# Three-pass products with the weight's low part last, and a mask moved from TensorE to VectorE

## The chip, the cores and the metric

The kernel runs on one core of one Trainium2 chip. The metric is device time in microseconds, as the median of several runs of the compiled program. The engines are TensorE (PE, with its weight loads shown apart as PEld), VectorE (DVE), ScalarE (ACT), GpSimd (POOL) and the queue that issues most DMAs (SP).

## The reference, cut to what matters

Two transformer blocks run one after the other on 256 tokens of width 1024, all in fp32. The first has a latent attention, a gated recurrence and a gated feed-forward; the second has two masked attentions of eight heads and an expert layer over 16,384 experts.

```
h = rms_norm(x, g_mix);  z = h @ w_in;  a = mla(...);  r = hgrn2(...)
x = x + concat([a, r]) @ w_o
x = x + (silu(rms_norm(x) @ w_gate) * (rms_norm(x) @ w_up)) @ w_down
x = x + sigmoid(rms_norm(x) @ w_ple_gate) * (p @ w_ple_proj)
...
x = x + hybrid_mixer(rms_norm(x))     # scores, causal mask, softmax, twice 8 heads
x = x + peer_ffn(rms_norm(x))         # every one of 128 x 128 expert rows is multiplied
out = rms_norm(x)
```

The mask keeps keys at or before the query; masked scores become minus infinity before the softmax.

## The kernel before, in words

Nearly all of the time goes to fp32 products that are made of three matmuls each in a faster format. Each operand is split into a high part (a rounded copy) and a low part (what the rounding left): `wh`, `wl` for the weight and `xh`, `xl` for the activations. The product is then wl·xh + wh·xl + wh·xh, summed in PSUM.

`unit` (L96) brings one block of a weight, mostly 512 KB: SP issues the load into `wraw`, ACT writes the high part `whi` (L107), and DVE, or POOL for some units, subtracts to give `wlo` (L112). For some units marked "add", ACT writes the negative of the high part and a DMA issued by POOL adds the raw weight (L109, L110). Each of the three buffers exists four times.

`mm3` (L118) issues the three matmuls of one step k in the order wl·xh (L120), wh·xl (L121), wh·xh (L122). `prodT` (L124) makes a tile of 128 outputs by 256 tokens from eight such steps, 24 matmuls in all, then calls `emit`, which reads the sum and often prepares the next layer's operands. `natural` (L147) does the same with tokens on the rows and up to 512 outputs per matmul (L152 to L154); `nat512` calls it with two steps per unit. `half` (L732, w_o), the products of the two branches in the second block, `w_down`, and `experts_in` (L1037, `expert_u`) call `mm3` themselves.

All engines run their instructions in the order in which the program issues them. Work beside the products (the recurrence, the attentions) is a set of generators that `tick` advances a few steps after each tile.

`Norm` (L182) collects the squares of a layer's output while it is made; `sums` (L211) adds them over the partitions by matmuls against two columns of ones (L216), and `spread` (L221) makes the inverse root available along the other axis. In a `prodT` with a `pre` list these two run after the first and the second tile. The first such products are w_in, the gate and up weights, w_ple_gate and w_pq.

The program starts with twelve products of ones (L261), issued before any data has come. Each fp32 product of whole precision shows as two matmul records.

In `attention` (L887), `scores` (L901) computes a head's scores for 128 queries by W keys (128 or 256): one fp32 product (L904), for the second attention two more for the decay (L906, L907), and one that adds the mask as identity times mask (L908). DVE takes the maximum (L910) and scales it (L911), and ACT takes the exponential out of PSUM (L913).

Of the kernel before, what the change touches and what calls it, by code (L numbers as in the profile page):

```python
# [9 lines left out]
F32R = mybir.dt.float32r  # L10
# [3 lines left out]
AF = mybir.ActivationFunctionType  # L14
OP = mybir.AluOpType
AX = mybir.AxisListType
# [3 lines left out]
T = 256  # L20
D = 1024
# [40 lines left out]
def body(tc, a, out, dbg=None):  # L62
    nc = tc.nc
    ctx = ExitStack()
    pool = lambda name, bufs=1, **k: ctx.enter_context(tc.tile_pool(name=name, bufs=bufs, **k))
# [6 lines left out]
    V = nc.vector  # L72
    S = nc.scalar
    G = nc.gpsimd
    PE = nc.tensor
# [48 lines left out]
    def prodT(name, n0, n1, kt, cols, x, emit, steps=0, pool=lambda u: False, pre=(), given=None):  # L124


        xh, xl = x
        held = []
        pre = list(pre)
        for u in range(n0, n1):  # L130
            wh, wl = given if given is not None and u == n0 else unit(a[name][u], (kt, cols), pool(u))
            for c in range(cols // 128):
                p = pmm()
                o = p[:, :T]
                s = slice(c * 128, (c + 1) * 128)
                for k in range(kt):
                    mm3(o, wh[:, k, s], wl[:, k, s], xh[:, k], xl[:, k], k == 0, k == kt - 1)
                held.append((u * (cols // 128) + c, o))
                if pre:
                    pre.pop(0)()  # L140
                if not pre:
                    for i in held:
                        emit(*i)
                    held = []
                tick(steps)

    def natural(p, wh, wl, x, j, kts, first, last, x0=0):  # L147

        xh, xl = x
        s = slice(j * 128, (j + 1) * 128)  # L150
        for k in range(kts):
            PE.matmul(p, xl[:, x0 + k, s], wh[:, k], start=first and k == 0, stop=False)  # L152
            PE.matmul(p, xh[:, x0 + k, s], wl[:, k], start=False, stop=False)  # L153
            PE.matmul(p, xh[:, x0 + k, s], wh[:, k], start=False, stop=last and k == kts - 1)  # L154

    def nat512(name, u0, x, emit, steps=0, pre=(), pool=lambda q: False):
        pj = [pmm(), pmm()]
# [19 lines left out]
    def rstd(r, v, ss, inv, eng=V):  # L177

        eng.tensor_scalar(v, ss, inv, EPS, op0=OP.mult, op1=OP.add)
        G.tensor_tensor(r, v, mhalf.to_broadcast([128, int(r.shape[1])]), op=OP.pow)  # L180

    class Norm:  # L182
# [25 lines left out]
        def make(self, bank):  # L208


            def sums():  # L211
                p = self.p = bank()
                for j in range(2):
                    js = slice(j * 128, (j + 1) * 128)
                    for i, sq in enumerate(self.parts):
                        PE.matmul(p[:, j * 2:j * 2 + 2], sq[:, js], ones[:, 0:2], start=i == 0, stop=i == len(self.parts) - 1)  # L216
                v = st.tile([128, 2], F32, name="nv", bufs=2)
                self.rn = res.tile([128, 2], F32, name="rnat", bufs=2)
                rstd(self.rn, v, p[:, 0:4:2], 1.0 / D)
# [26 lines left out]
    def cc(n):  # L246
        return cst[:, CC[n][0]:CC[n][1]]
# [7 lines left out]
    with tc.tile_pool(name="la", bufs=1) as la, tc.tile_pool(name="pa", bufs=1, space=PSUM) as pa:  # L255
        pax = lambda: pa.tile([128, 512], F32, name="ax", bufs=2)
        pay = lambda: pa.tile([128, 512], F32, name="ay", bufs=3)

        p = pay()
        for _ in range(12):  # L260
            PE.matmul(p[:, 0:128], ones, ones, start=True, stop=True)  # L261
        norm = Norm("g_mix")
        sqx = xb()

# [428 lines left out]
        prodT("w_in", 0, 4, 8, 128, h, emit_z, 4, pre=[steps[0], first_spread], given=unit0, pool=lambda u: u == 2)  # L693
# [38 lines left out]
        def half(k0, x, emit):  # L732
            for n in range(8):
                wh, wl = unit(a["w_o"][n][:, k0:k0 + 4], (4, 128))
                o = pmm()[:, :T]
                for k in range(4):
                    mm3(o, wh[:, k], wl[:, k], x[0][:, k], x[1][:, k], k == 0, k == 3)
                emit(n, o)
                tick(4)

# [72 lines left out]
    with tc.tile_pool(name="lb", bufs=1) as la, tc.tile_pool(name="pb", bufs=1, space=PSUM) as pb:  # L813
# [2 lines left out]
        pao = lambda: pb.tile([128, 512], F32, name="ao", bufs=1)  # L816
        nb = norm
        h = nb.h
        identr = la.tile([128, 128], F32R, name="identr")
        G.tensor_copy(identr, ident)  # L820
        negr = la.tile([128, 256], F32R, name="negr")
        G.tensor_copy(negr, cc("negmask"))
# [64 lines left out]
        def attention(b):  # L887

            q_, k_ = (qk["qa"], qk["ka"]) if b == 0 else (qk["qb"], qk["kb"])
            for j in range(2):  # L890
# [10 lines left out]
                def scores(hh):  # L901
                    rr = slice((hh % 2) * 64, (hh % 2) * 64 + 64)
                    p = psc()
                    PE.matmul(p[:, :W], q_[rr, hh // 2, js], k_[rr, hh // 2, :W], start=True, stop=False)  # L904
                    if b == 1:
                        PE.matmul(p[:, :W], cr[:, js], selr[:, hh, :W], start=False, stop=False)  # L906
                        PE.matmul(p[:, :W], selr[:, hh, js], crn[:, :W], start=False, stop=False)  # L907
# [85 lines left out]
    with tc.tile_pool(name="lp", bufs=1) as la, tc.tile_pool(name="pp", bufs=1, space=PSUM) as pb:  # L993
# [43 lines left out]
        def experts_in(c, how=False):  # L1037

            p = pmm()
            if how == "whole":  # L1040
                raw = st.tile([128, 8, 128], F32, name="wraw", bufs=4)
                nc.sync.dma_start(raw, a["expert_u"][c])
                for k in range(8):
                    PE.matmul(p[:, :T], raw[:, k], xf[:, k], start=k == 0, stop=k == 7)  # L1044
            else:
                hi, lo = unit(a["expert_u"][c], (8, 128), how)
                for k in range(8):
                    mm3(p[:, :T], hi[:, k], lo[:, k], xn[0][:, k], xn[1][:, k], k == 0, k == 7)
# [361 lines left out]
```

## Time and profile before

| what | value |
|---|---|
| median of 3 runs | 1461.62 us (1459.44 to 1462.62) |
| time of the profiled execution | 1456.88 us |
| its span, first to last instruction | 1455.1 us |
| PE busy | 1416.9 us, 97% |
| PEld busy | 1299.6 us, 89% |
| DVE busy | 1009.9 us, 69% |
| ACT busy | 763.4 us, 52% |
| POOL busy | 147.3 us, 10% |
| mean granted TensorE clock | 0.99 |

The busy time of PE holds ends that are modelled and overlap, so what PE does is read better from the distance between the starts of two matmuls. The granted clock is a share of full speed, 2.4 GHz; 0.50 is the lower of its two levels, 1.2 GHz. The profiled execution's own time is 4.74 us below the median of the runs.

### The profile page before, as it was taken

What the parts mean: (1) busy time and instruction counts of PE and PEld (TensorE: products, weight loads), DVE (VectorE), ACT (ScalarE), POOL (GpSimd) and SP (SyncE); (2) the same over time, 40 slices, a digit from 0 to 9 for tenths busy, and PEclk for the clock granted to TensorE, in tenths of its full rate; (3) what the DMA queues carried; (4) which work ended last, traced back from release to release, by engine and by line L of the source; (5) the groups of instructions that cost most, each with busy time, mean ns of one, the idle gap of its engine ahead of it and who ended that gap; (6) DMA issues with size and microseconds to landing.
All of it is one profiled execution on the core that took longest, in us unless ns stands there. A gap on an engine that the chain in (4) does not pass through costs nothing.

```text
span 1455.1 us, 25805 instructions
## 1 busy us (share of the span) xinstructions
PE 1416.9 (97%) x10238; PEld 1299.6 (89%) x10238; DVE 1009.9 (69%) x1792; ACT 763.4 (52%) x1182; POOL 147.3 (10%) x124
## 2 busy tenths in 40 slices
PE   8899999999999999899899999999999999999997
PEld 8796999999988889889899999899999998888886
DVE  6867877765765557796979995655555555577775
ACT  6764654444654444553257775555444444444443
POOL 4222200001100001367300000000000000000000
PEclk9999999999999999999999999999999999999999
DMA  7672566566554334645357777866676676797752
GB/s 232 165 203 59 165 193 187 188 180 190 161 169 132 115 108 142 200 132 160 116 200 250 246 247 258 277 206 210 195 221 215 222 214 192 230 293 217 220 185 92
DMA packets 104713, 275.98 MB, mean 190 GB/s; under 512 B 8464, under 2 KB 42000, under 8 KB 102416
## 3 DMA queue, kind: packets, MB, share of 16 engines
q1 hardware_dynamic: 100848, 252.31, 55.8%
q10 hardware_dynamic: 2304, 16.78, 3.1%
q0 software_dynamic: 1440, 5.24, 2.0%
q8 instruction: 80, 1.31, 0.4%
q14 instruction: 41, 0.34, 0.1%
HBM read 251.23 MB, written 17.83 MB: 185 GB/s over the span
## 4 chain that ended last, share of the span: by engine, by line
PE 84%; DVE 7%; ACT 3%; issue 3%; DMA 2%; POOL 1%; SPq 0%; POOLq 0%; ACTq 0%; DVEq 0%
PE mm L120 15%; PE mm L121 15%; PE mm L122 15%; PE ax L1233 8%; PE ax L1235 8%; PE ax L1234 8%; PE ax L1206 3%; PE mm L1044 2%; DVE wlo L112 1%; PE sc L904 1%; PE mm L152 1%; PE mm L154 1%; PE mm L153 1%; DVE hl L175 1%; DVE xnt L1062 1%
## 5 line engine op out<-in xcount | busy, mean ns | idle before, releaser
L112 DVE TENSOR_TENSOR wlo<-wraw,whi 128x1024 fp32r<-128x1024 f32 (+3 forms) x408 | 485.5, 1190 | 292.9 <-ACT whi L107 290.3
L107 ACT ACTIVATE whi<-wraw 128x1024 fp32r<-128x1024 f32 (+3 forms) x447 | 459.5, 1029 | 367.3 <-issue 158.1
L120 PE MATMUL mm<-hh,wlo 128*128 128x256 f32 x1928 | 548.7, 285 | 9.5 <-ACT hh L174 3.1
L121 PE MATMUL mm<-hl,whi 128*128 128x256 f32 x1928 | 541.7, 281 | 3.2 <-DVE hl L175 3.2
L122 PE MATMUL mm<-hh,whi 128*128 128x256 f32 x1928 | 540.5, 280 | 0.0
L120 PEld LDWEIGHTS mm<-hh,wlo 128*128 128x128 f32 x1928 | 365.0, 189 | 14.3 <-ACT hh L174 3.5
L121 PEld LDWEIGHTS mm<-hl,whi 128*128 128x128 f32 x1928 | 367.6, 191 | 7.8 <-DVE hl L175 4.5
L122 PEld LDWEIGHTS mm<-hh,whi 128*128 128x128 f32 x1928 | 365.4, 190 | 0.1
L1233 PE MATMUL ax<-whi,al 128*128 128x512 f32 x512 | 202.9, 397 | 0.5 <-DVE al L171 0.5
L1235 PE MATMUL ax<-whi,ah 128*128 128x512 f32 x512 | 202.6, 396 | 0.0
L1234 PE MATMUL ax<-wlo,ah 128*128 128x512 f32 x512 | 202.4, 395 | 0.0
L1050 ACT ACTIVATE hs<-mm 128x256 f32<-128x256 f32 x128 | 49.2, 384 | 159.4 <-PE mm L122 146.6
L1235 PEld LDWEIGHTS ax<-whi,ah 128*128 128x128 f32 x512 | 96.3, 188 | 22.9
L1233 PEld LDWEIGHTS ax<-whi,al 128*128 128x128 f32 x512 | 96.3, 188 | 21.0 <-PE mm L122 0.7
L1234 PEld LDWEIGHTS ax<-wlo,ah 128*128 128x128 f32 x512 | 96.4, 188 | 20.3
L112 POOL TENSOR_TENSOR wlo<-wraw,whi 128x1024 fp32r<-128x1024 f32 x29 | 73.0, 2525 | 216.7 <-ACT whi L107 216.6
L1249 POOL TENSOR_TENSOR ff<-fss 128x1 f32<-128x1 f32 x2 | 1.4, 698 | 730.9 <-ACT fsq L1244 730.9
L1199 DVE TENSOR_TENSOR oA<-one,g 128x3072 bf16<-128x3072 bf16 x32 | 56.0, 1755 | 0.6
L170 ACT ACTIVATE ah<-am 128x256 fp32r<-128x256 f32 x128 | 51.2, 401 | 5.0 <-DVE am L1222 5.0
L171 DVE TENSOR_TENSOR al<-am,ah 128x256 fp32r<-128x256 f32 x128 | 53.5, 418 | 0.2 <-ACT ah L170 0.2
L1206 PE MATMUL ax<-oA,one 128*128 128x128 bf16 x768 | 50.7, 219 | 1.6 <-DVE oA L1199 1.6
L122 PE MATMUL mm<-acth,whi 128*128 128x256 f32 x176 | 49.3, 280 | 0.0
(415 smaller groups left out, 1758.5 us busy)
## 6 DMA issues: line engine op xcount, KB each, us to landing
wraw<-in_expert_u_dram SPq DMA_DIRECT2D x128, 512.0 KB, 3.6
wraw<-in_expert_v_dram SPq DMA_DIRECT2D x128, 512.0 KB, 3.6
wraw<-in_w_gu_dram SPq DMA_DIRECT2D x44, 512.0 KB, 3.7
wraw<-in_w_in_nat_dram SPq DMA_DIRECT2D x24, 512.0 KB, 3.6
wraw<-in_w_down_dram SPq DMA_DIRECT2D x16, 512.0 KB, 3.6
wraw<-in_w_in_g_dram SPq DMA_DIRECT2D x16, 512.0 KB, 3.6
wraw<-in_w_pq_dram SPq DMA_DIRECT2D x16, 512.0 KB, 3.5
gd<-hh ACTq DMA_DIRECT2D x8, 1024.0 KB, 4.7
```

Of the source, the lines that this page charges most:

```text
L107: S.activation(hi[:, s], raw[:, s], AF.Copy)
L112: (G if pool else V).tensor_tensor(lo[:, s], raw[:, s], hi[:, s].bitcast(F32), op=OP.subtract)
L120: PE.matmul(o, wl, xh, start=first, stop=False)
L121: PE.matmul(o, wh, xl, start=False, stop=False)
L122: PE.matmul(o, wh, xh, start=False, stop=last)
L170: S.activation(hi, src, AF.Copy)
L171: V.tensor_tensor(lo, src, hi.bitcast(F32), op=OP.subtract)
L1199: V.tensor_tensor(A3, ow[:, :, 0:1].to_broadcast(s3), g3[:, qs].rearrange("p q k b -> p (q k) b")[:, :, None].to_broadcast([128, PAIRS * 3 ...
L1206: PE.matmul(p[:, i * 128:(i + 1) * 128], ow[:, q, 1, b::2], A3[:, q, k, b::2], start=k == 0, stop=k == 2)
L1233: PE.matmul(o, al[:, js], hi[:, ns], start=c == 0, stop=False)
L1234: PE.matmul(o, ah[:, js], lo[:, ns], start=False, stop=False)
L1235: PE.matmul(o, ah[:, js], hi[:, ns], start=False, stop=c == 127)
```

## The change

- `mm3s` takes all steps of a tile at once. In its usual order it runs wh·xh of all steps, then wh·xl of all steps, then wl·xh of all steps. With `x_late` it keeps the steps one after the other, as wh·xh, wl·xh, wh·xl.
- `prodT` uses `x_late` for the first tile of a product that has a `pre` list, and the usual order for every other tile. `half` uses `x_late` for its first tile. `experts_in` uses the usual order. `w_down`, the branch products and the forget gate keep `mm3`.
- `natural` runs xh·wh, then xl·wh, then xh·wl, each over all steps of the call.
- In the first tile of w_in, two products of ones follow each of the first seven steps.
- The sums of squares are taken against 128 columns of ones where two were used.
- The mask matmul and its two operands go. One `tensor_tensor_reduce` on DVE adds the mask to the scores out of PSUM, multiplies by -0.125, writes the result to `pe` and takes the row's minimum; ACT takes the exponential of `pe` in place.

```diff
+    def mm3s(o, steps, x_late=False, fill=None):
+        if x_late:
+            order = [(i, j) for i in range(len(steps)) for j in range(3)]
+        else:
+            order = [(i, j) for j in (0, 2, 1) for i in range(len(steps))]
+        for n, (i, j) in enumerate(order):
+            wh, wl, xh, xl = steps[i]
+            PE.matmul(o, (wh, wl, wh)[j], (xh, xh, xl)[j], start=n == 0, stop=n == len(order) - 1)
+            if fill is not None and j == 2 and i < len(steps) - 1:
+                fill()
...
+        late = len(pre) > 0
...
-                for k in range(kt):
-                    mm3(o, wh[:, k, s], wl[:, k, s], xh[:, k], xl[:, k], k == 0, k == kt - 1)
+                first = late and u == n0 and c == 0
+                mm3s(o, [(wh[:, k, s], wl[:, k, s], xh[:, k], xl[:, k]) for k in range(kt)], first, fill if first else None)
...
-        for k in range(kts):
-            PE.matmul(p, xl[:, x0 + k, s], wh[:, k], start=first and k == 0, stop=False)
-            PE.matmul(p, xh[:, x0 + k, s], wl[:, k], start=False, stop=False)
-            PE.matmul(p, xh[:, x0 + k, s], wh[:, k], start=False, stop=last and k == kts - 1)
+        for i, (xs, w) in enumerate(((xh, wh), (xl, wh), (xh, wl))):
+            for k in range(kts):
+                PE.matmul(p, xs[:, x0 + k, s], w[:, k], start=first and i == 0 and k == 0,
+                          stop=last and i == 2 and k == kts - 1)
...
-                        PE.matmul(p[:, j * 2:j * 2 + 2], sq[:, js], ones[:, 0:2], start=i == 0, stop=i == len(self.parts) - 1)
+                        PE.matmul(p[:, js], sq[:, js], ones, start=i == 0, stop=i == len(self.parts) - 1)
...
+        def busy(n=2):
+            for _ in range(n):
+                PE.matmul(warm[:, 0:128], ones, ones, start=True, stop=True)
...
-                for k in range(4):
-                    mm3(o, wh[:, k], wl[:, k], x[0][:, k], x[1][:, k], k == 0, k == 3)
+                mm3s(o, [(wh[:, k], wl[:, k], x[0][:, k], x[1][:, k]) for k in range(4)], n == 0)
...
-                    PE.matmul(p[:, :W], q_[rr, hh // 2, js], k_[rr, hh // 2, :W], start=True, stop=False)
+                    PE.matmul(p[:, :W], q_[rr, hh // 2, js], k_[rr, hh // 2, :W], start=True, stop=b == 0)
...
-                    PE.matmul(p[:, :W], identr, negr[:, 256 - W:], start=False, stop=True)
...
-                    V.tensor_reduce(mx, p[:, :W], AX.X, OP.max)
-                    V.tensor_scalar(mx, mx, -0.125, None, op0=OP.mult)
...
-                    S.activation(pe[:, :W], p[:, :W], AF.Exp, bias=mx, scale=0.125, accum_out=sm[:, hh:hh + 1])
+                    V.tensor_tensor_reduce(pe[:, :W], p[:, :W], cc("negmask")[:, 256 - W:], -0.125, 3.0e38, OP.add, OP.min, mx)
+                    S.activation(pe[:, :W], pe[:, :W], AF.Exp, bias=mx, scale=-1.0, accum_out=sm[:, hh:hh + 1])
```

## Rows read from the trace of the kernel before

**Rows 1.** Page, part 1: busy us, share of the span, instructions

```profile
PE 1416.9 (97%) x10238; PEld 1299.6 (89%) x10238; DVE 1009.9 (69%) x1792; ACT 763.4 (52%) x1182; POOL 147.3 (10%) x124
```

**Rows 2.** Page, part 4: chain that ended last, by engine

```profile
PE 84%; DVE 7%; ACT 3%; issue 3%; DMA 2%; POOL 1%; SPq 0%; POOLq 0%; ACTq 0%; DVEq 0%
```

**Rows 3.** Windows: stretch, busy us (instructions) of five engines, clock, DMA share, GB/s

```profile
460.00:550.00 90.00, 90.00 (x639) 77.90 (x638) 51.02 (x116) 39.00 (x84) 0.00 (x0) 1.00 0.35 110
...
550.00:583.00 33.00, 33.00 (x283) 33.00 (x283) 25.29 (x40) 14.72 (x21) 4.95 (x2) 1.00 0.49 157
...
594.00:612.00 18.00, 18.00 (x161) 18.00 (x160) 15.18 (x19) 11.64 (x21) 7.03 (x7) 1.00 0.63 192
...
700.00:745.00 45.00, 40.53 (x252) 37.63 (x252) 36.28 (x88) 12.98 (x25) 9.03 (x3) 0.96 0.43 141
745.00:892.00 147.00, 145.41 (x1627) 143.50 (x1626) 135.93 (x107) 108.57 (x136) 0.00 (x0) 1.00 0.71 240
```

**Rows 4.** Page, part 5: the costliest PE group; busy us, mean ns

```profile
L120 PE MATMUL mm<-hh,wlo 128*128 128x256 f32 x1928 | 548.7, 285 | 9.5 <-ACT hh L174 3.1
```

**Rows 5.** Timeline of PE: mask matmuls of the first, then the second attention

```profile
479.28 0.70 PE L904 MATMUL sc<-kaT,qaT 64*128 64x256 f32 x2
479.91 0.38 PE L908 MATMUL sc<-negr,identr 128*128 128x256 f32 x1
480.13 0.55 PE L898 MATMUL ao<-vv,PT 128*128 128x64 f32 x4
...
499.28 0.28 PE L907 MATMUL sc<-crn,selr 128*128 128x128 f32 x1
499.39 0.28 PE L908 MATMUL sc<-negr,identr 128*128 128x128 f32 x1
499.50 0.38 PE L898 MATMUL ao<-vv,PT 128*128 128x64 f32 x2
```

**Rows 6.** Groups by form, 460 to 550 us: the row maximum on DVE

```profile
L910 DVE TENSOR_REDUCE mx<-sc 128x1 f32<-128x256 f32 x16 | 6.7, 421 | 7.0 <-PE sc L908 7.0
```

**Rows 7.** Timeline: end of the first w_in tile, its sums, and its spread

```profile
12.02 0.87 DVE L175 SCALAR_TENSOR_TENSOR hl<-xa,vec,hh 128x256 fp32r<-128x256 f32 x2
...
13.64 0.28 PE L122 MATMUL mm<-hh,whi 128*128 128x256 f32 x1
...
13.90 1.03 PE L216 MATMUL ay<-ones,xb 128*128 128x2 f32 x8
14.79 0.36 PE L216 MATMUL ay<-ones,sqa 128*128 128x2 f32 x2
...
20.21 0.72 PE L223 MATMUL ay<-cst,rnat 128*128 128x128 f32 x4
20.68 0.37 PE L120 MATMUL mm<-hh,wlo 128*128 128x256 f32 x1
```

**Rows 8.** Windows around two drops of the granted clock

```profile
13.60:17.00 3.40, 3.40 (x32) 3.40 (x31) 1.77 (x3) 1.51 (x2) 2.78 (x2) 1.00 0.77 246
17.00:20.40 3.40, 3.40 (x18) 3.40 (x17) 1.99 (x2) 1.06 (x1) 1.34 (x1) 0.50 0.80 262
...
402.70:406.10 3.40, 3.40 (x11) 2.72 (x10) 0.37 (x1) 0.39 (x1) 0.94 (x1) 0.50 0.73 234
```

**Rows 9.** Timeline: waits of PE for a low part, early stages

```profile
31.92 0.36 PE L120 MATMUL mm<-hh,wlo 128*128 128x256 f32 x1 [0.95 <-DVE red L332]
...
63.15 0.51 PE L153 MATMUL mm<-wlo,hh 128*128 128x512 f32 x1 [3.23 <-DMA wlo<-wraw]
```

**Rows 10.** Timeline: waits of PE for POOL's low parts in the expert layer

```profile
709.11 7.67 POOL L112 TENSOR_TENSOR wlo<-wraw,whi 128x1024 fp32r<-128x1024 f32 x2 [7.75 <-ACT whi L107]
...
713.52 0.58 PE L120 MATMUL mm<-hh,wlo 128*128 128x256 f32 x1 [2.23 <-POOL wlo L112]
...
720.58 1.24 PE L1044 MATMUL mm<-xf,wraw 128*128 128x256 f32 x5
```

**Rows 11.** Timeline of PE: the first tile of w_out

```profile
586.33 0.28 PE L122 MATMUL mm<-hh,whi 128*128 128x256 f32 x1
589.29 0.50 PE L120 MATMUL mm<-hh,wlo 128*128 128x256 f32 x2 [2.69 <-ACT hh L174]
```

More of the change, by code (lines that the diff above doesn't have):

```diff
@@ L122, in mm3, with prodT @@
         PE.matmul(o, wh, xh, start=False, stop=last)
-    def prodT(name, n0, n1, kt, cols, x, emit, steps=0, pool=lambda u: False, pre=(), given=None):
+    def mm3s(o, steps, x_late=False, fill=None):
[8 more added lines that the diff above has]
+                fill()
+    def prodT(name, n0, n1, kt, cols, x, emit, steps=0, pool=lambda u: False, pre=(), given=None, fill=None):
         xh, xl = x
         held = []
+        late = len(pre) > 0
         pre = list(pre)
@@ L215, in sums @@
                     for i, sq in enumerate(self.parts):
-                        PE.matmul(p[:, j * 2:j * 2 + 2], sq[:, js], ones[:, 0:2], start=i == 0, stop=i == len(self.parts) - 1)
+                        PE.matmul(p[:, js], sq[:, js], ones, start=i == 0, stop=i == len(self.parts) - 1)
                 v = st.tile([128, 2], F32, name="nv", bufs=2)
                 self.rn = res.tile([128, 2], F32, name="rnat", bufs=2)
-                rstd(self.rn, v, p[:, 0:4:2], 1.0 / D)
+                rstd(self.rn, v, p[:, 0:T:128], 1.0 / D)
             def spread():
@@ L257, in body @@
         pay = lambda: pa.tile([128, 512], F32, name="ay", bufs=3)
-        p = pay()
-        for _ in range(12):
-            PE.matmul(p[:, 0:128], ones, ones, start=True, stop=True)
+        warm = pay()
+        def busy(n=2):
+            for _ in range(n):
+                PE.matmul(warm[:, 0:128], ones, ones, start=True, stop=True)
+        busy(12)
         norm = Norm("g_mix")
@@ L691, in emit_gz @@
             G.tensor_tensor(gz[:, j], gz[:, j], rows[:, 128:640], op=OP.mult)
-        prodT("w_in", 0, 4, 8, 128, h, emit_z, 4, pre=[steps[0], first_spread], given=unit0, pool=lambda u: u == 2)
+        prodT("w_in", 0, 4, 8, 128, h, emit_z, 4, pre=[steps[0], first_spread], given=unit0, pool=lambda u: u == 2, fill=busy)
         sides.append(tables())
@@ L818, in body @@
         h = nb.h
[L819 to L822, printed above, removed]
         selr = la.tile([128, 8, T], F32R, name="selr")
@@ L903, in scores @@
                     p = psc()
-                    PE.matmul(p[:, :W], q_[rr, hh // 2, js], k_[rr, hh // 2, :W], start=True, stop=False)
+                    PE.matmul(p[:, :W], q_[rr, hh // 2, js], k_[rr, hh // 2, :W], start=True, stop=b == 0)
                     if b == 1:
                         PE.matmul(p[:, :W], cr[:, js], selr[:, hh, :W], start=False, stop=False)
-                        PE.matmul(p[:, :W], selr[:, hh, js], crn[:, :W], start=False, stop=False)
-                    PE.matmul(p[:, :W], identr, negr[:, 256 - W:], start=False, stop=True)
+                        PE.matmul(p[:, :W], selr[:, hh, js], crn[:, :W], start=False, stop=True)
                     mx = la.tile([128, 1], F32, name="mx2", bufs=4)
-                    V.tensor_reduce(mx, p[:, :W], AX.X, OP.max)
-                    V.tensor_scalar(mx, mx, -0.125, None, op0=OP.mult)
                     pe = la.tile([128, T], F32, name="pe", bufs=3)
-                    S.activation(pe[:, :W], p[:, :W], AF.Exp, bias=mx, scale=0.125, accum_out=sm[:, hh:hh + 1])
+                    V.tensor_tensor_reduce(pe[:, :W], p[:, :W], cc("negmask")[:, 256 - W:], -0.125, 3.0e38, OP.add, OP.min, mx)
+                    S.activation(pe[:, :W], pe[:, :W], AF.Exp, bias=mx, scale=-1.0, accum_out=sm[:, hh:hh + 1])
                     return pe
@@ L1046, in experts_in @@
                 hi, lo = unit(a["expert_u"][c], (8, 128), how)
-                for k in range(8):
-                    mm3(p[:, :T], hi[:, k], lo[:, k], xn[0][:, k], xn[1][:, k], k == 0, k == 7)
+                mm3s(p[:, :T], [(hi[:, k], lo[:, k], xn[0][:, k], xn[1][:, k]) for k in range(8)])
             t = la.tile([128, T], F32, name="hs", bufs=HBUF)
```

## The prediction

> **What bounds the kernel now.** I read the page's busy times first, then the chain that ended last, then the windows stage by stage, and the timeline only where PE stands still. PE is busy 97% of the span and holds 84% of the chain [rows 1, 2]; DVE comes second with 69% and 7%. The reader should see in the windows that this isn't an average over unlike stages: in 460 to 550 us, 550 to 583 and 594 to 612 PE is busy for the whole stretch at clock 1.00, and in 745 to 892 for 145.41 of 147 us [rows 3]. There an earlier low part is worth nothing, because no one waits for it. The change can save only three things: matmuls taken out of a full stretch, waits of PE at the seams, and stretches at clock 0.50. Each is priced below against the profiled execution, 1456.88 us, which is 4.74 us under the median of 1461.62; I carry the difference over to the median unchanged.
>
> **The mask.** It is one matmul per head and query block: 2 attentions x 2 blocks x 8 heads = 32. In the first attention with 256 keys the mask takes 480.13 - 479.91 = 0.22 us of PE from start to start; in the second, 499.50 - 499.39 = 0.11 us [rows 5]. Part of the 0.22 is the first matmul of one format behind another, and where a three-part product follows, that product then pays it. So the ends are 32 x 0.11 = 3.5 and 32 x 0.22 = 7.0 us; I take 0.14 in the mean, -4.5 us. PE is full in this stretch [rows 3], so all of it shows. On DVE a reduction of 0.42 us over 256 keys and a small multiplication go [rows 6] and one fused instruction comes, of which the trace has no row. Nearest is that reduction: it reads the same scores once. I take 0.42 us; below, nothing less than the shorter form of 128 keys is likely, and above I allow twice, 0.84. Even then 32 x 0.42 = 13 us on DVE lie in 90 us of which DVE uses 51 [rows 3], so PE hides it. ACT still waits for one DVE result; its source is now SBUF, and it uses 39 of the 90 us. The Trainium skill ("VectorE: DVE Perf Modes", section "Two Vector instructions with no wait between them") says that an instruction which writes out its accumulator counts as two, the main one and an accumulator read; no run here shows it on DVE, and by it the fused instruction would leave DVE about as busy as now and the sum as it is.
>
> **Products of ones in the first tile.** Seven steps get two each, 28 records. Four records of a 128-wide fp32 product take 20.68 - 20.21 = 0.47 us at full clock [rows 7], so they take 7 x 0.47 = 3.3 us, and some format changes. The tile waits for the activations: the last two low parts end at 12.02 + 0.87 = 12.89, and the last matmul starts at 13.64 [rows 7]. Only the fills behind that point can delay; one tail of about a step and a half remains, with the stretch at full clock in exchange for half. I take +0.7 us; the ends are 0 (all inside waits) and +3.3 (all behind).
>
> **Sums 128 wide.** Eight records 2 wide take 14.79 - 13.90 = 0.89 us, 0.11 each; four records 128 wide take 0.47, 0.12 each [rows 7]. The width is nearly free: 52 records in six norms x 0.01 = +0.3 us (0 to 0.5). What it can give back is clock. From 13.6 to 17.0 PE is busy throughout, yet from 17.0 to 20.4 the clock is 0.50, the lower level of 1.2 GHz [rows 8]; what PE did before it fell is the two-wide sums, from 13.9 us on [rows 7]. If the clock stays up with the wide sums, half of 3.4 us comes back: -1.7. The Trainium skill ("TensorE: Matmul & The Clock Gate", Part 1, section "What's actually happening") says that the throttled state is the default and that activity releases it; the trace agrees in so far as the next drop, at 402.7 us, also follows a wait. The drop at 402.7 us [rows 8] comes behind the same kind of sums, but also behind a real wait, which stays; half a chance, -0.8.
>
> **Low part last.** Each of three waits shortens by the work that can run ahead of it. (a) At 31.92 PE has waited 0.95 us at a new tile [rows 9]; the named releaser is a table operation on DVE, but the matmul's operand is a low part. Sixteen matmuls can now go first, about 16 x 0.115 = 1.8 us: -1.0. (b) At 63.15 it waited 3.23 us for a low part that a DMA adds [rows 9]. In `natural` four 512-wide matmuls precede the low part, one of which ran already; three at 0.23: -0.7. (c) POOL takes 7.67 us for two low parts from 709.11, and PE stands until 713.52 and reaches the next kind of work at 720.58 [rows 10]. New: the first unit's 16 matmuls run during POOL's first, its last 8 end at 714.4; the second's 16 end at 716.3, its low part is there at 709.11 + 7.67 = 716.8, and its 8 end at 717.7: -2.9, including the half clock that follows the wait now. What is late next is the row of whole-precision products behind, which is PE's own, so the gain is kept until 745, and DVE (36 of 45 us busy there [rows 3]) has the room.
>
> **What it costs.** The first tile of w_out has no `pre` list, so it gets the usual order. Its last activation comes late: PE stops at 586.33 after 21 of 24 matmuls and goes on at 589.29 when ACT has written it [rows 11]. Now wh·xh of the eighth step is the eighth matmul. PE will stop after 7, wait for the same ACT instruction, and then owe 17 rather than 3: 14 x 0.115 = +1.6 us. The longer wait may also hold the clock down before 590.5: +0.4. I take +2.0; ends +0 (the activation comes in time) and +3.3 (a further 3.4 us at half clock).
>
> **Sum.** -4.5 + 0.7 + 0.3 - 1.7 - 0.8 - 1.0 - 0.7 - 2.9 + 2.0 = -8.6 us. The profiled time goes to 1448.3, the median to **1453.0 us** (-0.6%). With every term at its better end the median would be about 1447; at its worse end, with nothing back from the clock and 1 us from the three waits, about 1464.
>
> **Rivals.** *The early gains are given back* (20%). Waits before 160 us and at 709 us belong to side chains on DVE, ACT and POOL; if these end last anyway, PE merely waits elsewhere. Mask, fills, wide sums and w_out remain: -4.5 + 0.7 + 0.3 + 2.0 = -1.5, 1460.1 us. For it: DVE is busy 36 of 45 us at 700 to 745 [rows 3]. Against: PE alone is full behind each of these seams.
>
> *The slow pitch takes over* (10%), which is the slower side. PE has two paces for the same work: 33.00 / 283 = 0.1166 us per record in 550 to 583, 18.00 / 161 = 0.1118 in 594 to 612, both at clock 1.00 and PE full [rows 3]. The rows don't say what sets it. The fast one stands behind a wait at 589, the slow one in an unbroken stream; an order that streams more evenly could leave the fast one. Three lines of 1928 and smaller groups [rows 4] make some 6,300 records; if half run fast now and all turn slow, 3,150 x 0.0048 = +15 us: 1468 us. It outweighs the gain from 8.6 / 0.0048 = 1,800 records on. Against it: both paces occur with the same order, so the order is not what chooses.
>
> *The fast pitch takes over* (8%): the same price the other way, 1438 us. The same argument speaks against it.
>
> *The order changes nothing* (12%), because low parts come too late even for the sixteenth matmul: then (a) to (c) shrink to about 1 us, while mask and clock stay: 1456.6 us. Against: in (c) POOL's row gives the end of the low part, and it is inside the cover for the first unit.
>
> **How the numbers follow.** The forecast has 50%, its own range 1448 to 1457 us. About 0.2% (2.9 us) is what a measurement of this kernel can tell from no change: 1458.7 to 1464.5 counts as the same. Faster: 50 + 8 + 10 of the 12 + 4 of the 20 = 72%. Same: 14 of the 20 + 2 + 3 of the slow pitch = 19%. Slower: 7 + 2 = 9%. The range from 1441 to 1461 leaves out the slow pitch and most of the fast one.
>
> **What would show it.** Right: no L908-like records between L904 and what follows, and the two attentions shorter by 4 to 5 us; clock 1.00 from 17 to 20 us; the seam at 711 us without a wait ahead of the high parts; in w_out's first tile a wait after 7 matmuls, about as long as the present one plus 1.6 us. Wrong: a start-to-start distance in the long streams (176 to 365 us, 910 to 1300) that differs from now by more than 1 ns, or DVE instructions in the attentions that PE waits for.

## The result, and the profile after

The changed kernel takes **1441.56 us** (median of 4 runs, 1438.63 to 1444.94) beside 1462.01 for the kernel before, a ratio of 0.9868, 95% interval [0.985, 0.9886]; a second set gave 0.9881 [0.9858, 0.9904]. The forecast was 1453.0. The direction was right. The time lies just inside the range from 1441 to 1461 that the prediction gives last, and outside 1448 to 1457, the range of the forecast itself: the gain is 20 us (17 by the ratio of the second set) where 8.6 were forecast.

The profiled execution after took 1444.94 us with a span of 1443.2, which is 11.9 us under the profiled execution before. The two profiles alone would have shown little more than half of the gain: the one before was better than the median of its kernel, the one after worse. The granted clock of each execution explains most of that, and more than half of the gain that the forecast missed.

**What the stages show.** First the totals, part 1 of the page after:

```profile
PE 1408.4 (98%) x10234; PEld 1292.5 (90%) x10234; DVE 989.2 (69%) x1792; ACT 770.6 (53%) x1182; POOL 146.2 (10%) x122
```

PE is still the bound, DVE no busier [rows 1]. Windows inside the same stages as [rows 3], some of another length:

```profile
430.00:520.00 90.00, 90.00 (x644) 78.84 (x645) 50.50 (x130) 43.54 (x91) 0.00 (x0) 1.00 0.40 126
520.00:569.00 49.00, 49.00 (x406) 47.07 (x405) 33.25 (x60) 22.02 (x35) 4.95 (x2) 1.00 0.45 135
590.00:597.50 7.50, 7.50 (x68) 7.50 (x67) 6.07 (x9) 5.19 (x9) 2.84 (x3) 1.00 0.67 196
686.00:731.00 45.00, 42.83 (x274) 40.10 (x273) 36.79 (x103) 15.32 (x26) 7.88 (x3) 0.96 0.46 151
731.00:878.00 147.00, 145.52 (x1635) 144.07 (x1634) 135.42 (x105) 110.43 (x136) 0.00 (x0) 1.00 0.70 240
```

PE is full where it was full. In the seam of the expert layer (686 to 731) it is now busy 42.83 of 45 us, where it was 40.53. That this shortens the layer as a whole isn't so; the part on the prediction has the stages around it.

The attentions, timeline of PE as in [rows 5], and the new instruction on DVE by form, 430 to 540 us:

```profile
441.19 0.49 PE L917 MATMUL sc<-kaT,qaT 64*128 64x128 f32 x2
441.61 0.33 PE L931 MATMUL pt<-cst,pe 128*128 128x128 f32 x1
...
491.20 0.27 PE L920 MATMUL sc<-crn,selr 128*128 128x128 f32 x1
491.31 1.15 PE L133 MATMUL mm<-hh,whi 128*128 128x256 f32 x8
```

```profile
L924 DVE CUSTOM_DVE_ANT_0 pe<-sc,cst 128x256 f32<-128x256 f32 x16 | 6.7, 419 | 2.2 <-PE sc L917 1.6 <-PE sc L920 0.5
...
L924 DVE CUSTOM_DVE_ANT_0 pe<-sc,cst 128x128 f32<-128x128 f32 x16 | 4.5, 288 | 0.3
...
L924 DVE DVE_READ_ACCUMULATOR2_ANT mx<- 128x1 f32 x32 | 2.7, 84 | 0.0
```

No mask record follows the scores. From the first scores to the first branch product the two attentions take 121.65 us before and 116.50 after. The fused instruction takes 0.419 us over 256 keys, as the reduction of [rows 6] did. It counts as two, as the rule of the Trainium skill ("VectorE: DVE Perf Modes", section "Two Vector instructions with no wait between them") had it: the trace agrees, with an accumulator read of 0.084 us.

The first tile, and the windows of [rows 7, 8] with one more, at 50.5 us:

```profile
14.12 1.10 PE L133 MATMUL mm<-hh,whi 128*128 128x256 f32 x8
...
15.18 0.38 PE L230 MATMUL ay<-ones,sqa 128*128 128x128 f32 x2
15.40 1.06 PE L230 MATMUL ay<-ones,xb 128*128 128x128 f32 x8
```

```profile
13.60:17.00 3.40, 3.40 (x32) 3.40 (x32) 2.71 (x2) 2.52 (x3) 2.47 (x1) 1.00 0.92 290
17.00:20.40 3.40, 2.88 (x26) 2.69 (x25) 2.64 (x6) 0.21 (x1) 1.66 (x1) 1.00 0.82 302
50.50:53.90 3.40, 3.40 (x12) 2.91 (x12) 2.77 (x8) 1.92 (x3) 0.00 (x0) 0.50 0.52 154
400.00:403.40 3.40, 3.27 (x29) 3.08 (x29) 2.85 (x10) 1.01 (x3) 0.00 (x0) 1.00 0.54 157
```

Both priced drops are gone: 17.0 to 20.4 and 400 us stand at 1.00, and so does all between 53.9 and 576. The one at 50.5 stays; from 576 us to the last stage there are four stretches of 3.4 us where the profile before has three.

The waits, in the order of [rows 9 to 11]: the low part that a DMA adds, POOL and PE at the expert seam, and w_out.

```profile
61.69 0.73 PE L167 MATMUL mm<-wlo,hh 128*128 128x512 f32 x2 [2.25 <-DMA wlo<-wraw]
...
568.62 0.85 PE L133 MATMUL mm<-hh,whi 128*128 128x256 f32 x6
570.08 2.03 PE L133 MATMUL mm<-hh,whi 128*128 128x256 f32 x15 [0.61 <-ACT hh L188]
574.54 0.39 PE L133 MATMUL mm<-hh,whi 128*128 128x256 f32 x1 [2.43 <-ACT hh L188]
...
695.29 1.86 PE L133 MATMUL mm<-hh,whi 128*128 128x256 f32 x8 [2.17 <-ACT hs L1061]
```

```profile
696.54 4.14 POOL L112 TENSOR_TENSOR wlo<-wraw,whi 128x1024 fp32r<-128x1024 f32 x1 [6.38 <-ACT whi L107]
```

The wait at 31.92 is gone, the one at 63.15 went from 3.23 to 2.25 us, and PE no longer waits for POOL at the expert seam; the wait of 2.17 us for ACT's `hs` ahead of it was there before (2.24) and stays. In w_out PE stops for 0.61 us after six products and for 2.43 after 21, not for long after 7: the 21 high products in a row are those of the first seven steps of *three* tiles, so the order of issue sends the work of two more tiles ahead of the first tile's eighth step.

### The profile page after: what moved, and what is told of

The parts are those of the page before. It is cut to its first block, busy times and chain, and to the rows that moved or that the text cites. A ratio compares the mean times of both kernels' runs of the same rounds, so it can differ in the third digit from the quotient of the medians.

```text
span 1443.2 us, 25863 instructions
## 1 busy us (share of the span) xinstructions
PE 1408.4 (98%) x10234; PEld 1292.5 (90%) x10234; DVE 989.2 (69%) x1792; ACT 770.6 (53%) x1182; POOL 146.2 (10%) x122
## 4 chain that ended last, share of the span: by engine, by line
PE 50%; DVE 3%; DMA 2%; issue 1%; ACT 1%; POOL 0%; POOLq 0%; ACTq 0%; DVEq 0%; SPq 0%
PE mm L133 22%; PE ax L1246 8%; PE ax L1244 8%; PE ax L1245 8%; PE ax L1217 3%; PE mm L1056 1%; DMA gd<-hl 1%; DMA wraw<-in_expert_u_dram 0%; DMA hh<-gd 0%; DVE wlo L112 0%; PE ax L1031 0%; DVE one L1207 0%; DVE cand L1106 0%; DVE tk L1024 0%; DVE pick L1026 0%
## 5 line engine op out<-in xcount | busy, mean ns | idle before, releaser
L133 PE MATMUL mm<-hh,whi 128*128 128x256 f32 x1920 | 277.9, 284 | 5.2 <-ACT hh L188 3.0
L133 PE MATMUL mm<-hl,whi 128*128 128x256 f32 x1920 | 269.9, 280 | 1.3 <-DVE hl L189 1.3
L133 PE MATMUL mm<-hh,wlo 128*128 128x256 f32 x1920 | 266.5, 279 | 0.0
L133 PEld LDWEIGHTS mm<-hh,whi 128*128 128x128 f32 x1920 | 249.1, 189 | 13.3 <-ACT hh L188 3.6
L133 PEld LDWEIGHTS mm<-hl,whi 128*128 128x128 f32 x1920 | 243.4, 190 | 2.1 <-DVE hl L189 2.1
L133 PEld LDWEIGHTS mm<-hh,wlo 128*128 128x128 f32 x1920 | 241.8, 189 | 0.2 <-DVE wlo L112 0.2
L1245 PEld LDWEIGHTS ax<-wlo,ah 128*128 128x128 f32 x512 | 96.6, 189 | 20.4
L121 PE MATMUL mm<-actl,whi 128*128 128x256 f32 x176 | 49.3, 280 | 0.0
```

The lines of the kernel that those rows point to most:

```text
L133: PE.matmul(o, (wh, wl, wh)[j], (xh, xh, xl)[j], start=n == 0, stop=n == len(order) - 1)
L1245: PE.matmul(o, ah[:, js], lo[:, ns], start=False, stop=False)
```

## What the clock takes, execution by execution

Every timed execution has a span and a mean granted clock. A stretch at 0.50, the level of 1.2 GHz, costs about half its length where PE is busy (512-wide matmuls start 0.24 us apart ahead of the drop at 402.7 us of the first profile, and 0.43 behind it), so (1 - clock) x span is about what an execution loses to it, and the remainder is what it would take at full clock. The clock is given to 0.001, so one execution is known to 0.7 us; the remainder scatters by 2 to 3 us among executions of one kernel, so a mean over six to twelve of them by about 1 us. Every profile also has its last 3 to 5 us at 0.50, behind PE's last product; this adds some 2 us to each loss and nothing to a difference. Means over all timed executions:

| kernel | runs | ratio to before, 95% | lost to the clock, us | remainder, us |
|---|---|---|---|---|
| before | 79 | 1 | 18.6 | 1439.8 |
| mask only (`m_mask`) | 12 | 0.9975 [0.9955, 0.9996] | 17.8 | 1435.9 |
| order only (`o_order`) | 12 | 1.0002 [0.9981, 1.0022] | 20.5 | 1437.2 |
| wide sums and ones only (`c_clock`) | 12 | 0.999 [0.9972, 1.0008] | 14.1 | 1443.5 |
| mask, order (`a_neither`) | 8 | 0.9945 [0.9921, 0.9968] | 19.4 | 1431.7 |
| mask, order, ones (`a_nowide`) | 8 | 0.9948 [0.993, 0.9966] | 16.1 | 1434.1 |
| mask, order, wide (`a_nofill`) | 6 | 0.9915 [0.9894, 0.9936] | 12.8 | 1432.4 |
| mask, wide, ones (`a_noorder`) | 12 | 0.9956 [0.9939, 0.9973] | 12.6 | 1438.0 |
| order, wide, ones (`a_nomask`) | 6 | 0.9927 [0.99, 0.9954] | 9.4 | 1437.7 |
| all, order behind 175 us only (`a_early`) | 6 | 0.9927 [0.9899, 0.9954] | 12.5 | 1434.2 |
| all, order up to 175 us only (`a_latter`) | 7 | 0.9923 [0.9895, 0.9951] | 12.0 | 1435.0 |
| **all: the changed kernel** (two sets) | 9 | 0.9868 and 0.9881 | 9.1 | 1430.9 |

So the change takes 9.5 us out of the clock's loss and 8.9 out of the remainder; the forecast had -2.5 and -6.1. The profiled execution before had a clock of 0.990, a loss of 14.6, which is 4.0 less than the mean. The 4.74 us between it and the median of its first runs, whose own clocks aren't on record, were thus most likely clock too.

## The experiments

The expectations number four theories: 1, the pace of the records (113 or 118 ns) is drawn anew in each execution; 2, the new order sets it; 3, the edits for the clock bring the gain by themselves; 4, they need the new order too.

**The kernels as they are** (`r_before`, `r_after`), no edit.

> The kernel before, unchanged, for a second profile. Theory 1 (the pace of 113 or 118 ns per 256-wide matmul is drawn anew in every execution): the same time within 0.2%, but the stretch of the gate and up products (w_gu, 123.0 us from its first sums to the first w_down matmul in the first profile, all at 118 ns) may come out near 119 us, and other streams at another pace than before. Theory 2 (the order of the matmuls sets the pace): the same time, and w_gu again at 118 ns and 123 us.

> The changed kernel, unchanged, for a second profile. Theory 1: 0.986 of before within 0.2%, and w_gu at either pace, 119 or 123 us, independent of the first profile's 119 us. Theory 2: w_gu again at 113 ns and 119 us, as in the first profile of this kernel, because its matmuls run high parts first.

Measured: 1.0011 [0.9994, 1.0029] and 0.9881. Windows at 0.50 of the repeated kernel before, then those of the repeated changed kernel at about the same times:

```profile
10.60:20.80 10.20, 10.09 (x45) 9.79 (x46) 5.86 (x10) 5.74 (x10) 4.74 (x3) 0.50 0.81 293
51.60:58.40 6.80, 6.80 (x25) 6.05 (x25) 6.73 (x9) 4.86 (x8) 0.04 (x1) 0.50 0.20 63
143.70:150.50 6.80, 6.80 (x25) 5.03 (x24) 1.72 (x4) 1.56 (x6) 0.00 (x0) 0.50 0.13 42
...
406.60:413.40 6.80, 6.80 (x20) 5.64 (x21) 2.41 (x4) 0.94 (x2) 2.96 (x4) 0.50 0.55 166
```

```profile
10.60:20.80 10.20, 10.07 (x85) 9.93 (x86) 7.87 (x14) 5.91 (x10) 3.83 (x3) 1.00 0.83 297
49.40:52.80 3.40, 3.40 (x12) 2.92 (x11) 2.77 (x8) 1.66 (x2) 0.00 (x0) 0.50 0.50 154
143.70:150.50 6.80, 6.20 (x47) 5.71 (x46) 4.81 (x11) 3.63 (x9) 2.04 (x2) 1.00 0.00 0
...
406.60:413.40 6.80, 6.80 (x44) 5.92 (x42) 5.48 (x14) 4.36 (x6) 0.00 (x0) 1.00 0.35 114
```

The kernel before loses more to the clock than its first profile showed: 10.2 us at 0.50 from 10.6 where that had two times 3.4, and 6.8 us at 143.7 where that had none. The pace of the records at full clock, which two rivals were about, differs between executions of one program. The same stretch in the two profiles of the changed kernel:

```profile
180.00:290.00 110.00, 110.00 (x973) 110.00 (x972) 76.91 (x123) 58.95 (x83) 0.00 (x0) 1.00 0.64 194
```

```profile
180.00:290.00 110.00, 110.00 (x937) 110.00 (x937) 73.45 (x117) 57.11 (x80) 0.00 (x0) 1.00 0.59 186
```

One program, both at clock 1.00 and without a gap, and 110 / 973 = 113 ns or 110 / 937 = 117 ns a record. The order does not fix it: in the gate and up products the fast pace stands in 8 of 12 profiles with the new order there and in 2 of 6 with the old (118.5 to 119.1 us for the stage beside 122.9 to 123.4, half-clock time taken out). Whether the order shifts the odds, 18 profiles can't tell.

**One part alone.** `m_mask` has the mask edit on the kernel before, `c_clock` the wide sums and the ones on the old order, `o_order` the new order alone (its diff, shortened; the other two are the same lines the other way):

```diff
 # o_order = changed kernel
-V.tensor_tensor_reduce(pe, p, negmask, -0.125, ...)
+PE.matmul(p, identr, negr) ... V.tensor_reduce(mx, p) ... V.tensor_scalar(mx, mx, -0.125)
-PE.matmul(p[:, js], sq[:, js], ones, ...)
+PE.matmul(p[:, j * 2:j * 2 + 2], sq[:, js], ones[:, 0:2], ...)
-prodT("w_in", 0, 4, ..., fill=busy)
+prodT("w_in", 0, 4, ...)
```

> The kernel before with the mask edit alone. The prediction's term is -4.5 us (0.997). The two profiles differ by 7.2 us from the first sums of the second block's norm to the first branch product (162.0 against 154.8), which would be 0.995 if it were all the mask's. Theory 1 and theory 2 agree here; a rival is that the mask saves only the distance from start to start, 3.5 us.

> The kernel before with the new order of products alone (all steps with the high part first, low part last, first tiles step by step), with the old mask, two-wide sums and no products of ones in the first tile. Theory 1: the waits for low parts go and w_out's first tile loses, -2.6 us by the prediction's terms (-1.0 - 0.7 - 2.9 + 2.0), 0.998. Theory 2: the order also sets the fast pace in the streams that it rules (w_gu 4 us, the expert products 3 to 5 us), -10 to -14 us, 0.991 to 0.993.

> The kernel before with the 128-wide sums and the products of ones in the first tile, nothing else (old order, old mask). Theory 3 (most of the gain is time at the lower clock that these two edits avoid in the first 65 us): 10 to 13 us off, 0.991 to 0.993, with at most two stretches of 3.4 us at clock 0.50 before 65 us, where the second profile of the kernel before has 10.2 us from 10.6 and 6.8 us from 51.6. Theory 4 (the new order is needed too, since without it PE waits for the low part in the first tiles): 2 to 4 us off, 0.998. The prediction's terms for the two together: +0.7 + 0.3 - 1.7 - 0.8 = -1.5 us, 0.999.

Measured: 0.9975, 1.0002 and 0.999, so two of the three parts bring nothing alone. The mask is as forecast: its remainder is 3.9 us less, and from its first to its last scores the first attention shrinks from 44.12 to 39.79 us. The theory that the order sets the pace falls, and so does the one that the clock edits bring 10 us by themselves.

**One part undone** in the changed kernel (`a_noorder`: the old order throughout; `a_nowide`; `a_nofill`; `a_neither`; `a_nomask`), with the lines of the diffs above.

> The changed kernel with the old order of products (low part of the weight first, step by step), keeping mask, wide sums and products of ones. Theory 3: the order is worth little, as when it was made alone (1.0002): 14 to 17 us off the kernel before, 0.989. Theory 4: it lacks the part that makes the others work, about 6 us off, 0.996.

> The changed kernel with the sums of squares two columns wide again. Theory 3: a stretch at clock 0.50 comes back behind the first sums (17 to 20 us in the first profile of before) and in part of the runs behind the others: 2 to 5 us slower than the changed kernel, 0.990 to 0.992 of before. Rival: the products of ones alone hold the clock, 0.988 as the changed kernel.

> The changed kernel without the products of ones in the first tile. Theory 3: the clock is at 0.50 from about 10 us for 7 to 14 us, as in all four profiles without them: 4 to 7 us slower than the changed kernel, 0.991 to 0.993 of before. Rival, the prediction's term: 0.7 us faster than the changed kernel, 0.987.

> The changed kernel with the sums of squares 2 wide again and without the products of ones in the first tile: the mask edit and the new order are left. Theory 4 (the order pays only where the first 180 us also keep the clock, for which both the wide sums and the products of ones are needed): the mask edit's own ratio is left, 0.9975 x 1.0002 = 0.998, about 1457 us, and the first sums of the gate and up products start at 182 us or later, with 17 us or more at clock 0.50 ahead of them. Rival (the order does its work by itself, by the waits it takes away, and the wide sums and the ones each hit only a drop of their own): at or below the ratio without the wide sums, 0.9948, so 1449 to 1453 us. Theory 1 (the 113 or 118 ns pace is drawn anew in every execution) expects either pace in the gate and up products.

> The changed kernel with the mask as a matmul again, as before. If the mask's part is only the 32 matmuls: 4 us more than the changed kernel, a ratio of 0.9905 to 0.991 to the kernel before, (1 - clock) x span unchanged at about 9 us. Rival (the mask's matmuls and their two operands, made on POOL, hold up more than themselves, since mask and order alone gave 0.9975 and 1.0002 and both together 0.9945): 0.993 or more.

Given the others, the wide sums are worth 0.9881 / 0.9948 = -0.67%, the ones -0.34%, the order -0.75%, each known to about 0.3%. Alone the order brought nothing, nor did the sums and the ones together (each of these two alone was not run): the parts work together. `a_noorder` went to theory 4, `a_nofill` as theory 3 had it, `a_nowide` lost about 10 us where 2 to 5 were expected. `a_neither` went to the rival (0.9945; I expected 0.998). Without the mask edit the remainder is 6.8 us more (forecast 4) and the clock's loss as in the changed kernel; 0.9927 lies between the two expectations.

What the wide sums give back is not what was priced. The profile of `a_nowide` has two-wide sums, but neither priced drop (timeline of its first sums, then two windows):

```profile
15.06 1.03 PE L230 MATMUL ay<-ones,xb 128*128 128x2 f32 x8
```

```profile
17.00:20.40 3.40, 3.30 (x27) 3.09 (x28) 2.59 (x4) 1.45 (x2) 1.64 (x1) 1.00 0.91 341
401.40:404.80 3.40, 3.40 (x18) 2.89 (x19) 1.54 (x3) 1.02 (x2) 1.77 (x2) 1.00 0.61 187
```

Beside the changed kernel it loses to the clock elsewhere: 13.7 us at 0.50 from 47.0, and 3.4 at 183.5, behind the sums of the gate and up products, where 5 of the 6 profiles with two-wide sums have such a drop and 2 of the 12 with wide ones.

What stands against the order where the sums are two wide is in the traces, too. In each of the three profiles that have the new order and two-wide sums, PE waits at 45 to 50 us for a low part that a DMA adds. `a_nowide`, timeline and the window behind it:

```profile
45.27 1.20 PE L133 MATMUL mm<-hh,wlo 128*128 128x256 f32 x8 [2.62 <-DMA wlo<-wraw]
```

```profile
47.00:60.70 13.70, 13.70 (x58) 12.93 (x58) 11.69 (x19) 10.68 (x14) 2.01 (x1) 0.50 0.43 149
```

`o_order` waits 3.07 us at 50.17 and has 13.7 us at 0.50 behind it, `a_neither` 3.25 at 47.08 and 17.1. The profiles with the new order and wide sums have no wait there and, the two kernels with other w_in_kr products (below) aside, 3.4 to 6.8 us at 0.50 between 45 and 60 us. With the sums' width the issue order of other instructions around them changes, too; that this moves the wait is what the traces show, which of the moved instructions does it isn't settled. The other way round there is a trace of it, too: the three profiles with the old order ahead of 175 us and wide sums wait 0.81 to 0.96 us at 42 to 43 us for such a low part, and the three with the old order and two-wide sums don't.

**The order by stages** (the diff is shortened; `natural` has the same switch).

```diff
+    old = [True]                       # a_early; [False] in a_latter
     def mm3s(o, steps, x_late=False, fill=None):
+        if old[0]:
+            order = [(i, j) for i in range(len(steps)) for j in (1, 2, 0)]
...
+        old[0] = False                 # ahead of w_gu; True in a_latter
         prodT("w_gu", 0, 44, ...)
```

> The changed kernel with the order of before in all products ahead of the gate and up products (the first 175 us), the new order behind. If the order works by keeping the clock in the first 180 us (theory 4): the gain of the order is lost nearly whole, a ratio of 0.994 to 0.9955 to the kernel before, 1451 to 1454 us, and (1 - clock) x span is 12 us or more against 9.1 in the changed kernel. Rival (the order earns its part behind 550 us, in the waits for low parts in the expert layer): 0.989 to 0.9905, 1444 to 1446 us, with clock losses as in the changed kernel.

> The changed kernel with the new order in the first 175 us and the order of before behind. Theory 4: most of the gain stays, a ratio of 0.989 to 0.9905 to the kernel before; the stages show what the profile of the kernel before had there: 1.5 us more in the stage of the one-hot products and about 4 in the whole experts less 1 to 3 in the stages beside them. Rival (the order earns its part in the expert layer): 0.994 or more.

Measured: 0.9927 and 0.9923, so each theory holds for about half. The early order is worth 12.5 - 9.1 = 3.4 us of clock and 3.3 of remainder, the later one 2.9 and 4.1. What goes with the early part's clock is plain in the profiles. First the timeline of PE and the window behind it in `a_early`, then both in `a_latter`:

```profile
141.30 0.63 PE L676 MATMUL ay<-cst,pr 128*128 128x128 f32 x4 [1.87 <-DVE pr L672]
```

```profile
142.20:149.00 6.80, 6.80 (x22) 4.73 (x22) 2.04 (x5) 1.72 (x6) 0.00 (x0) 0.50 0.14 39
```

```profile
136.85 0.63 PE L676 MATMUL ay<-cst,pr 128*128 128x128 f32 x4 [0.30 <-DVE pr L672]
```

```profile
142.20:149.00 6.80, 6.20 (x47) 5.72 (x45) 4.26 (x9) 3.33 (x8) 1.70 (x2) 1.00 0.00 0
```

All six profiles with the old order ahead of 175 us have the wait of 1.87 or 1.88 us; five have 6.8 us at 0.50 behind it. All twelve with the new order there have 0.29 or 0.30, and none has the drop behind it. The sixth is the first profile of the kernel before, timeline and window:

```profile
141.17 0.63 PE L650 MATMUL ay<-cst,pr 128*128 128x128 f32 x4 [1.88 <-DVE pr L646]
```

```profile
142.20:149.00 6.80, 6.80 (x50) 5.76 (x50) 2.77 (x7) 3.43 (x10) 0.49 (x1) 1.00 0.13 42
```

So the drop goes with the wait, but doesn't always follow it: there the wait was to be seen, the drop was not. Of the later part the stages show less than the timed 4.1: from the first scores of the expert layer to its last stage the repeated changed kernel takes 288.87 us and `a_latter` 290.19, each with one stretch of 3.4 us at 0.50. The whole experts take 52.14 beside 55.42 and the one-hot products 138.93 beside 140.49, but 3.5 us come back in the stages between. Where the remaining 2 to 3 us lie, if they aren't scatter, is open.

**Three ways to go further**: w_in_kr's 64-wide products 128 wide (`v_kr`), w_out's first tile step by step (`v_late`), both (`v_best`), and ones ahead of the low part waited for at 59 us (`v_fill`).

```diff
-            natural(p[:, :64], wh, wl, h, j, 8, True, True)
+                    n = 128 if k < 7 else 64
+                    PE.matmul(p[:, :n], xs[:, k, js], w[:, k * 64:k * 64 + n], ...)   # v_kr
-        prodT("w_out", 0, 8, 8, 128, mg, emit_o2, pool=lambda u: u < 2)
+        prodT("w_out", 0, 8, 8, 128, mg, emit_o2, pool=lambda u: u < 2, late=True)    # v_late
+            for _ in range(8):
+                PE.matmul(q[:, 0:128], ones, ones, start=True, stop=True)             # v_fill
```

> The changed kernel with the 64-wide products of w_in_kr 128 wide in seven of eight steps; the 64 columns more are not read by anyone. In all ten profiles so far the clock falls to 0.50 at 47 to 54 us, right behind these products. If their narrowness lowers the clock, as with the 2-wide sums: no stretch at 0.50 between 45 and 60 us, 3.4 us of it gone, so 1.7 us less, 0.9988 of the changed kernel. Rival (the clock falls for the waits around them, for the mean over all products there, or at that time in any case): the stretch stays and the time is that of the changed kernel or up to 0.5 us more.

> The changed kernel with the first tile of w_out step by step (high times high, low weight, low activation), as the tiles with a list of sums have it. In the changed kernel PE stands still at 569.19 and 571.83 us for 0.61 and 2.43 us for ACT's last high part of the activations, with 7 high products behind it; step by step 18 to 21 products fit ahead of that wait. If the wait is a loss of its own: the wait falls to about 1 us or less and the time by 1.6 to 2 us, 0.9988 of the changed kernel. Rival (the loss is hidden, since the stage from the end of the second attention to the sums behind w_out takes 30.5 us against 30.9 before): the same time within 0.1%.

> The last two edits together on the changed kernel. If both are losses of their own they add up: 1.7 + 1.7 = 3.4 us less, 0.9977 of the changed kernel, about 1437.7 us and a ratio to the kernel before of 0.986. Rival: the same as the changed kernel, 0.988, within 0.1%.

> The changed kernel with eight 128-wide products of ones (16 records, 1.9 us) in the second unit of the first token-major products, ahead of its low weight part, for which PE waits 2.25 us at 59.05 us. If waits lower the clock: the stretch at 0.50 at about 50 us stays, since it lies ahead, but none at 60 to 75 us comes as in four of the other profiles; the time is the changed kernel's or up to 1.7 us less, 0.987 to 0.988. If the ones come behind the wait's end because the low part lands earlier in other executions: up to 1.9 us more, 0.9895. No theory expects more than 0.9895.

None beats the changed kernel. `v_late` gave 0.9896 [0.9875, 0.9917]: its wait is 2.69 us where 3.04 stood, and the rival held as far as the interval tells: 27 products stand ahead of the wait where 21 did, but PE waits for the same instruction of ACT either way. `v_kr` gave 0.9936 [0.9912, 0.996], `v_best` 0.991 [0.9892, 0.9928]: the drop at 50 us went, but PE now waits longer a little later (`v_kr`, timeline and window):

```profile
66.12 1.22 PE L167 MATMUL mm<-wlo,hh 128*128 128x512 f32 x2 [5.95 <-DMA wlo<-wraw]
```

```profile
62.00:72.20 10.20, 6.08 (x16) 4.76 (x17) 8.11 (x17) 6.21 (x9) 3.39 (x4) 0.50 0.73 171
```

The drop at 46 to 53 us is in all 16 profiles with the 64-wide products and in neither of the two with wide ones. But the edit moved other work as well, as the wait of 5.95 us shows, so whether the narrow products lower the clock stays open. `v_fill` gave 0.9895 [0.9866, 0.9923]; the ones fill the wait whole, and the clock falls ahead of it, as without them, and at 113.8 us (timeline and windows):

```profile
60.55 1.95 PE L735 MATMUL mm<-ones 128*128 128x128 f32 x16
```

```profile
49.00:55.80 6.80, 6.80 (x23) 5.83 (x23) 6.17 (x13) 4.32 (x6) 0.00 (x0) 0.50 0.23 77
...
113.80:120.60 6.80, 6.80 (x15) 4.08 (x15) 4.31 (x6) 1.42 (x2) 0.00 (x0) 0.50 0.24 77
```

## Why the prediction was wrong, and where it was right

- **The failed step is the clock**, priced at -1.7 - 0.8 = -2.5; it brought 18.6 - 9.1 = 9.5 us. The prediction priced two drops of one profile and put them down to the two-wide sums. Both did go, but `a_nowide` lacks them with its two-wide sums, so their width alone doesn't make them. The wide sums are worth 16.1 - 9.1 = 7.0 us of clock given the other parts, and the profiles show them elsewhere, at 47 and 183 us. What was missed besides: the drop at 10 us, which the ones take (it is in all six profiles without them, and in two of twelve with them, there 3.4 us each); the one at 143, which goes with the 1.88 us wait that the order takes; and that the one profiled execution had less of them than most. The "next drop, at 402.7 us" was a misreading: the profile before has one at 51.2 between the two.
- **"I carry the difference over to the median unchanged"** failed with it. Of the 4.74 us most were probably half-clock time (14.6 us lost against 18.6), the very thing that the change removes.
- **The mask** was right in kind and about in size: -4.5 forecast; -3.9 alone, -5.15 by the two attentions' stages, -6.8 given the other parts; DVE is hidden as argued.
- **The waits (a) to (c)** are right only in part. (a) is gone in all twelve profiles with the new order ahead of 175 us. (b) went from 3.23 to 2.25 us in the first two profiles, which looks like the forecast, but by luck: in the repeated ones (timeline of `r_before`, then `r_after`) it is longer with the new order.

```profile
64.65 0.50 PE L153 MATMUL mm<-wlo,hh 128*128 128x512 f32 x1 [1.44 <-DMA wlo<-wraw]
...
60.85 0.73 PE L167 MATMUL mm<-wlo,hh 128*128 128x512 f32 x2 [2.57 <-DMA wlo<-wraw]
```

- **The rival "The early gains are given back"** (20%) holds for (c) by its mechanism. The wait for POOL is gone, and the whole experts take 53.77 and 52.14 us from their first to their last product where they took 56.30 and 56.16. But from the first scores of the expert layer to the first product of its last stage the two profiles before take 290.96 and 290.73 us, those of the changed kernel 292.17 and 288.87, which is no shorter beyond the scatter. Its time of 1460.1 was missed because of the clock. PE waits elsewhere, for instance for DVE's `al` at the head of the last stage (timeline of the first profile before, then after; 0.73 and 1.60 us in the repeated ones):

```profile
909.32 0.47 PE L1233 MATMUL ax<-whi,al 128*128 128x512 f32 x1 [0.53 <-DVE al L171]
...
895.82 0.47 PE L1244 MATMUL ax<-whi,al 128*128 128x512 f32 x1 [3.06 <-DVE al L185]
```

- **The order's remainder**, -7.1 given the other edits, is more than the -4.6 of (a) to (c), but saved waits don't explain it: all waits of PE over 0.15 us add up to 30.0 and 25.5 us in the two profiles before, 28.2 in `a_noorder`, and 26.7 and 26.0 in those of the changed kernel, with the 1.6 us at 141, which had no term, among them. Some 5 of the 7.1 us stay open; the two paces may have a part in them.
- **w_out's +2.0** was wrong. "PE will stop after 7" took the source order of one tile; the issue order puts three tiles' high products there, and the two waits are 3.04 us where one was 2.69 [rows 11]. The 21 of 24 before was misread as well: 27 products of w_out precede that wait, some of them of another tile.
- **The costs +0.7 and +0.3** don't show in the changed kernel: its remainder is no more than that of `a_neither` (1430.9 and 1431.7). On the old order the same edits raise the remainder by 2.1 to 3.7 us; 0.8 to 1.0 of that is the wait at 42 to 43 us, the rest is open.
- **The pitch rivals**: both paces occur in every profile. That the time came near the 1438 us of the fast pitch is chance; the clock took half of the gain. **"The order changes nothing"** held for the order alone, by another mechanism than late low parts at the waits (a) to (c): a new wait of 3 us and the half clock behind it.

## What to carry to other kernels

Read the clock of every timed execution, and profile the kernel twice, before pricing an edit: (1 - clock) x span tells how typical that profile is, and the distance between its time and the median can be the very loss that the edit touches. Where PE waits 1 to 3 us, price what the clock may lose behind it beside the wait. Check a wait that went by the length of the stage around it, since PE may wait elsewhere. And when two edits bring nothing alone, look for the wait that each leaves to the other.

## What the runs showed of the hardware

- A wait of 1.88 us was followed by 6.8 us at clock 0.50 in five of six profiles, and waits of 2.6 to 3.3 us at 45 to 50 us went with 13.7 to 17.1 us, where profiles without such a wait have 3.4 to 6.8: the stretch at 1.2 GHz costs more than the wait. Not every wait does this: nothing stands behind the 3.23 us at 63.15 of [rows 9], nor behind the 2.25 and 2.57 us in the two profiles of the changed kernel.
- The same program runs its full-clock records at 113 or 117 ns, some 4 us between the two over the gate and up products (119.05 and 125.03 us, of which 1.7 are half clock in the slower one).
- In the first tile the ones, which do nothing but keep PE at work, take the drop away in ten of twelve profiles. The Trainium skill ("TensorE: Matmul & The Clock Gate", Part 1, section "What's actually happening") says that activity releases the throttled state, and there the trace agrees. It doesn't at 50.5 us in the changed kernel: PE runs without a gap from 37.8 us on, from 44.5 to 49.8 with products 64 wide, and the clock falls all the same, as it does at 46 to 53 us in 16 of the 18 profiles.
